# The query's low part on all 128 partitions: score products of two attentions in a two-layer trunk step

## The chip, the cores and the metric

The kernel runs on one core of a Trainium2 chip, as one launch. The metric is device time in microseconds (us), the median of three runs. Engines are named as the profile does: PE is TensorE's matrix products, PEld its loads of the stationary operand, DVE VectorE, ACT ScalarE, POOL GpSimd, SP the queue that issues the DMAs. L78 is line 78 of the kernel before.

## What is computed

One step through two layers of a diffusion backbone: 512 sample tokens and 128 prompt tokens, 1024 channels, float32. Each layer runs four token mixers side by side (a gated linear recurrence, grouped-query attention, neighbourhood attention, latent attention), merges them through gates, and ends in a feed-forward network. The change touches the scores of two of the mixers. Of the reference:

```python
# neighbourhood attention: 8 heads of 64, a window of the sample plus 256 cached keys
s_loc = jnp.einsum('brqhd,brjkhd->bhrqjk', qg, kg).astype(jnp.float32) * NA_SCALE
s_ctx = jnp.einsum('brqhd,bphd->bhrqp', qg, k_ctx).astype(jnp.float32) * NA_SCALE
...
# latent attention: 8 heads, 64 channels made from a latent and 32 rotary ones shared by the heads
k = jnp.concatenate([kv[..., :ML_NOPE],
                     jnp.broadcast_to(k_rope[:, :, None, :], (B, T, ML_HEADS, ML_ROPE))], axis=-1)
...
s = jnp.einsum('bqngd,bknd->bngqk', qblk, k).astype(jnp.float32) * scale
p = jax.nn.softmax(s, axis=-1).astype(v.dtype)
```

## The kernel before

**Two parts.** PE multiplies a rounded form of float32 (`F32R`), so every operand is kept as a high part (the rounded value) and a low part (what the rounding left). A projection is three products, `hi*hi`, `hi*lo` and `lo*hi`, summed in PSUM (`gemm`, and `part`, which gives it out in steps).

**Scores.** A head has 64 channels, half of the 128 partitions. `k_pair` (L480) keeps a head's keys as one tile `kp` (`nkp` in the neighbourhood attention, `mkp` in the latent one): high part on its own 64 partitions, low part on the other 64. `split_q` (L199) keeps the query's high part on both halves (`nqd`, `mqd`, one tile per head; the second half is a copy by DVE, L206), and the low parts of the two heads together in one tile (`nql`, `mqlo`): head A's on partitions 0 to 63, head B's on 64 to 127. `pair_scores` (L485) then makes two products per range of keys: the high part against both parts of the keys, a sum over 128 partitions, and the low part against the keys' high part, over 64. The latent attention adds a third, over 128 partitions, for the rotary channels (`kr`, `mqrr`). In grouped-query attention (`gkA`, `gq`) both products of a range of keys run over 128 partitions.

**An attention pair.** `attn_pair` (L243) works on two heads in nine units: the prompt of both heads, then per head four tiles of 128 queries. A unit's scores go to `pss`, the only buffer of its kind (two PSUM banks); DVE takes the maximum, ACT the exponential, DVE the division. Later steps transpose the probabilities on PE (`pst<-ident,P`), split them (`ph`, `pl`) and multiply by V. Neighbourhood units have 256 or 384 keys of the window and 256 cached ones, latent units 768 (512 and 256); the prompt unit has 128.

**Order.** A layer runs 16 such steps: four latent pairs, four recurrence heads, four neighbourhood pairs, four grouped-query pairs. `weave` (L1074) puts, between the steps of the pair under way, pieces of other work in proportion to given lengths: the preparation of the next pair (its projections and splits) and gates and merges (`psg` products). From what this program order says, the framework's scheduler makes the order of each engine, which holds at run time. `psg` has three buffers, `wraw` (weights as loaded) two.

**SBUF.** `Arena` hands out slots of two sizes, 38 of 640 columns and 19 of 896; of the free ones it takes the one that has been free longest, and a 640 tile takes a large slot when no small one is free. A tile in a reused slot waits for the last reader of the tile before it. No DMA is issued from POOL.

The lines that matter most:

```python
            self.split(q[a, cols], ql[a, cols], src[a], scale)          # split_q, per head
            self.nc.vector.tensor_copy(q[b, cols], self.r(q[a, cols]))
...
        self.mm(S[:, o : o + n], qd[half][:, qc], kp[half][:, k0 : k0 + n], True, False)
        self.mm(S[:, o : o + n], ql[a, qc], kp[half][a, k0 : k0 + n], False, last)
```

Of the kernel before, what the change touches and what calls it, by code (L numbers as in the profile page):

```python
# [8 lines left out]
F32R = mybir.dt.float32r  # L9
# [5 lines left out]
PSUM = bass.MemoryType.PSUM  # L15
# [5 lines left out]
GW = 64  # L21
# [13 lines left out]
class Arena:  # L35
    """Slots of SBUF handed out in program order, the longest free one first."""
# [28 lines left out]
class Trunk:  # L65
# [7 lines left out]
    # ---------------------------------------------------------------- basics  # L73
# [30 lines left out]
    def wload(self, src, a, b, joined=False, kept=None):  # L104
        """Both parts of a weight, each [128, a, b]; joined: side by side, [128, a, 2 b];
        kept: a list that gets the tiles, from the arena."""
# [20 lines left out]
    def gemm(self, w, xs, c0, c1, ms=slice(0, 128), k0=0):  # L127
        """PSUM [m, c1-c0] of one column range; xs = (hi, lo) tiles by k."""
        hi, lo = w
        m = ms.stop - ms.start  # L130
        ps = self.psg()
        o = ps[:m, 0 : c1 - c0]
        n = len(xs)
        for k in range(n):
            self.mm(o, hi[:, k0 + k, ms], xs[k][0][:, c0:c1], k == 0, False)
            self.mm(o, hi[:, k0 + k, ms], xs[k][1][:, c0:c1], False, False)
        for k in range(n):
            self.mm(o, lo[:, k0 + k, ms], xs[k][0][:, c0:c1], False, k == n - 1)
        return o

    def part(self, w, xs, c0, c1):
        """gemm, in steps of 8 products, negative: inside one product; the last step is the caller's."""
# [11 lines left out]
    def fm(self, src, name, scale=1.0):  # L154
        """Feature-major projection of one block of 128 columns, as float32."""
# [7 lines left out]
    def flip(self, t, c0, c1, rows=128):  # L163
        """Blocks of 128 columns c0..c1 of t transposed, side by side in PSUM."""
# [6 lines left out]
    # ------------------------------------------------------- splits into parts  # L171
    def split(self, hi, lo, src, scale=1.0):
        """hi = round(src*scale), lo = src*scale - hi."""
# [7 lines left out]
    def split_stack(self, dst, src, half, scale=1.0):  # L181
        """src rows of head `half` (64 partitions) -> dst stacked [hi;lo] or [lo;hi]."""
# [4 lines left out]
    def split_dup(self, dst, src, half, cols):  # L187
        """dst = (hi, lo), each on both halves of the partitions."""
# [10 lines left out]
    def split_q(self, qd, ql, src, cols, scale):  # L199
        """qd: per head, hi on both halves; ql: [lo A; lo B]."""  # L200
        for half in range(2):
            a = slice(64 * half, 64 * half + 64)
            b = slice(64 - 64 * half, 128 - 64 * half)
            q = qd[half]
            self.split(q[a, cols], ql[a, cols], src[a], scale)
            self.nc.vector.tensor_copy(q[b, cols], self.r(q[a, cols]))  # L206

    # ---------------------------------------------------------------- attention
    def softmax(self, S, P, p0, n1, n2, bias):
        """Probabilities of the scores S[:, 0:n1] (+ bias) and S[:, 512:512+n2] to P from  # L210
        column p0 on; the part that has a bias first when p0 says so."""
# [24 lines left out]
    def add_halves(self, dst, pv):  # L236
        """dst [64, n] = rows 0-63 of pv + rows 64-127."""
# [5 lines left out]
    def attn_pair(self, scores, plan, vst, frees):  # L243
        """Two heads, prompt and sample, in steps: the scores of one query tile, the transposes of
        the tile before, the products with V of the one before that; returns the output,
        feature-major. scores(S, half, t) writes the scores of query tile t; plan[g] = (V tiles by
        column of P, per query tile (first column, columns, ...)); frees[half] goes with the head."""
# [103 lines left out]
    def v_tile(self, vst, src, t0):  # L351
        """src [128 keys, n tiles x 2 heads x 64] -> V per head, [128 keys, tile, hi|lo]."""
# [6 lines left out]
    def v_split(self, vst, t, cache):  # L359
        """V of t, feature-major, and of the cache, token-major; tiles 0-3 sample, 4-5 cache, 6 prompt."""  # L360
# [17 lines left out]
    # ------------------------------------------------------------------- GQA  # L378
    def gqa_normed(self, l, blk, g, cost):
        """Block of two heads, token-major: normalised, gained, rotated (sample)."""  # L380
# [82 lines left out]
    def rope(self, out, x, nb, nf, cos, sin):  # L463
        """out, x [128, nb*2*nf], pairs interleaved; cos, sin [128, nb, nf]."""
# [14 lines left out]
    # ------------------------------------------------- neighbourhood attention  # L479
    def k_pair(self, kp, src, cols):  # L480
        """kp: head A [hi;lo], head B [lo;hi]."""
# [3 lines left out]
    def pair_scores(self, S, o, qd, ql, kp, half, qc, k0, n, last):  # L485
        a = slice(64 * half, 64 * half + 64)
        self.mm(S[:, o : o + n], qd[half][:, qc], kp[half][:, k0 : k0 + n], True, False)
        self.mm(S[:, o : o + n], ql[a, qc], kp[half][a, k0 : k0 + n], False, last)

    def na_pair(self, l, i, c):  # L490
# [21 lines left out]
        ql = self.u("nql", F32R)  # L512
# [23 lines left out]
        # P by columns: (cache, 0, 1, 2) and (1, 2, 3, cache)  # L536
        plan = (((4, 5, 0, 1, 2), ((0, 4, 256, 256, 256, 0), (0, 5, 384, 256, 256, 0))),
                ((1, 2, 3, 4, 5), ((0, 5, 384, 256, 0, 384), (1, 5, 256, 256, 128, 384))))
        frees = [[kp[0], vst[0], qd[0]], [kp[1], vst[1], qd[1], ql]]
        return lambda: self.attn_pair(scores, plan, vst, frees)  # L540

    # ------------------------------------------------------------------- MLA
    def mla_pre(self, l):
        """Compressed latents: normalised query latent, keys' latent, rotary parts."""
# [3 lines left out]
        # the projections, first columns of all first  # L548
        raw3 = [self.u("mfm") for _ in range(4)]
        for c0, c1 in HALVES:  # L550
# [4 lines left out]
            # both parts of the weights side by side  # L555
# [58 lines left out]
        # rotary key: rows [hi; hi; lo; lo]  # L614
# [27 lines left out]
        # rotary part of the queries, token-major  # L642
# [18 lines left out]
    def mla_pair(self, l, i, c):  # L661
# [5 lines left out]
        # rotary queries of the two heads, rows [hi; lo; hi; lo]  # L667
# [17 lines left out]
        ql = self.u("mqlo", F32R)  # L685
# [8 lines left out]
        if i % 2 == 0:  # L694
            # values of this pair and the next one
# [27 lines left out]
        frees = [[kp[0], vst[0], qd[0], qr[0]], [kp[1], vst[1], qd[1], qr[1], ql] + ([kr] if i == 3 else [])]  # L723
        return lambda: self.attn_pair(scores, FULL, vst, frees)

    # ------------------------------------------------------------------- HGRN
    def hgrn_head(self, l, h, c):
        nc, A = self.nc, self.A

        def evac(fn, dst, ps, c0, c1):  # L730
            """column order (col, row) of the sample -> row-major; prompt as it is."""
# [15 lines left out]
        # Blocks of w tokens, at first one. Per direction: T, the decay of each block; queries by the  # L747
        # decay since the block's edge; keys by that up to it. Kept by turns: of forward and backward
        # what the products of this level take, and the other one.
# [16 lines left out]
        # value, token-major in row order  # L766
# [6 lines left out]
        # output gate, feature-major in token order  # L773
# [12 lines left out]
    def hgrn_mix(self, l, h, Q, T, qs, ks, kk, v, sg):  # L786
        nc, A = self.nc, self.A
        blk = [slice(c * 128, (c + 1) * 128) for c in range(5)]
        # pair matrix At[s, t], level by level
# [10 lines left out]
        for lev in range(7):  # L800
# [7 lines left out]
            # of four blocks the outer ones keep their direction on the next level, the inner ones  # L808
            # change it; on the last level all blocks end up with one direction
# [24 lines left out]
        # T: [128, 5] decay of each chunk; states chunk by chunk  # L834
# [51 lines left out]
    # ------------------------------------------------------------------ merge  # L886
    def gate(self, l, n, d, gates, away=False):
        """tanh of half the gate, branch n, block d."""
# [29 lines left out]
    # ------------------------------------------------------------------ adaLN  # L918
    def silu(self, c):
        """silu of both conditions, kept as rows in DRAM."""  # L920
# [8 lines left out]
    def ada_first(self, c):  # L929
        """Blocks 0..15 of layer 0, weights moving; loads x and starts on the first columns' norm."""  # L930
# [15 lines left out]
    def ada_chunk(self, l, q, c):  # L946
        """Blocks 4q..4q+3 of layer l on TensorE, the weights moving."""
# [18 lines left out]
    def ada_tail(self, l, b0, b1, parts, depth, last=False):  # L966
        """Blocks b0..b1 of layer l, weights by channel, one part of the sum after the other:
        mod[l][:, b] = silu(cond) w + b."""
# [33 lines left out]
    # --------------------------------------------------------------- main norm  # L1002
    def rstd_rows(self, x, c0, c1):
        """x: 8 tiles; returns a tile [128, c1-c0], every row 1/rms of the tokens c0..c1."""
# [529 lines left out]
```

## Time and profile before

| | us |
|---|---|
| median of three runs (lowest, highest) | 3252.76 (3247.86, 3254.46) |
| the profiled execution, first to last instruction | 3253.3 |
| PE busy | 3155.2 (97%) |
| PEld busy | 2956.6 (91%) |
| DVE busy | 2179.9 (67%) |
| ACT busy | 1457.7 (45%) |
| POOL busy | 290.5 (9%) |

The profiled execution has no other time than its span; it lies 0.5 us above the median. Busy time is the union of an engine's instructions. Products on PE overlap, since one starts while the one before it drains, so what a product costs in a row of products is read from start to start, not from its duration. The span divides into stages, by the first and last score products: latent attention 128 to 360 us, recurrence to 634, neighbourhood attention to 865, grouped-query attention to 1080, then merge, output projection and feed-forward network; the second layer's four mixers stand at 1740, 1972, 2212 and 2443.

### The profile page before, as it was taken

The numbers are of one execution on the slowest core, as the hardware profiler recorded it, in microseconds if no ns is written. First come the engines' busy times: TensorE is split into PE (matmuls) and PEld (weight loads), VectorE is DVE, ScalarE is ACT, GpSimd is POOL, SyncE is SP. The second block draws the span as 40 slices with busy tenths as digits, with TensorE's granted clock in tenths as the row PEclk, the third lists the DMA queues.
The fourth block names the chain that finished last, engine by engine and source line by source line (L and its number), as shares of the span: only waits on it lengthen the run. The fifth ranks groups of instructions, "written<-read, shape, count | busy, mean of one in ns | idle before, by whom it ended". The sixth has DMA issues, their size and how long they took to land.

```text
span 3253.3 us, 54150 instructions
## 1 busy us (share of the span) xinstructions
PE 3155.2 (97%) x20898; PEld 2956.6 (91%) x20898; DVE 2179.9 (67%) x4830; ACT 1457.7 (45%) x3086; POOL 290.5 (9%) x301
## 2 busy tenths in 40 slices
PE   8999998999999999999999999999999999999998
PEld 4888988888889999999997889998888999999998
DVE  5675888877777577777867666677677766533334
ACT  4554433455666352121355544445566644422222
POOL 1100222110111010000001002231001100000000
PEclk9999999999999999999999999999999999999999
DMA  6111243232111345444521112213221124322222
GB/s 211 63 54 57 86 129 113 88 95 87 49 40 58 107 139 173 149 153 150 158 99 58 48 58 78 71 53 98 86 71 43 39 62 148 106 82 74 79 72 72
DMA packets 135121, 297.16 MB, mean 91 GB/s; under 512 B 15888, under 2 KB 53584, under 8 KB 134864
## 3 DMA queue, kind: packets, MB, share of 16 engines
q1 hardware_dynamic: 134864, 293.71, 28.6%
q8 instruction: 165, 2.70, 0.3%
q14 instruction: 92, 0.75, 0.1%
HBM read 276.70 MB, written 16.95 MB: 90 GB/s over the span
## 4 chain that ended last, share of the span: by engine, by line
PE 74%; DVE 10%; issue 10%; ACT 3%; DMA 2%; POOL 1%; DVEq 0%; POOLq 0%; SPq 0%; ACTq 0%
PE psg L78 57%; PE pss L78 10%; PE pst L78 3%; PE pst L81 3%; DVE trash L984 2%; DVE wlo L123 1%; PE pst L167 1%; DMA ada<-in_w_ada 1%; ACT P L234 1%; DVE hA L804 1%; DVE hq L819 0%; DVE pl L176 0%; DVE sm L217 0%; ACT ph L84 0%; DVE P L231 0%
## 5 line engine op out<-in xcount | busy, mean ns | idle before, releaser
L78 PE MATMUL psg<-hh,whi 128*128 128x384 f32 (+1 forms) x3776 | 1128.4, 317 | 5.9 <-ACT whi L84 2.8
L78 PE MATMUL psg<-hl,whi 128*128 128x384 f32 (+1 forms) x3776 | 1112.9, 312 | 4.4 <-DVE hl L1061 2.9
L78 PEld LDWEIGHTS psg<-hh,whi 128*128 128x128 f32 x3776 | 717.6, 190 | 13.5 <-ACT whi L84 3.2
L78 PEld LDWEIGHTS psg<-hl,whi 128*128 128x128 f32 x3776 | 717.8, 190 | 9.6 <-DVE hl L1061 5.0
L78 PE MATMUL psg<-hh,wlo 128*128 128x384 f32 (+1 forms) x3744 | 653.1, 314 | 0.0
L84 ACT ACTIVATE whi<-wraw 128x1024 fp32r<-128x1024 f32 (+3 forms) x402 | 380.0, 947 | 470.2 <-PE psg L78 387.3
L78 PEld LDWEIGHTS psg<-hh,wlo 128*128 128x128 f32 x3744 | 572.4, 191 | 2.2
L123 DVE TENSOR_TENSOR wlo<-wraw,whi 128x1024 fp32r<-128x1024 f32 (+3 forms) x398 | 452.6, 1138 | 125.7 <-ACT whi L84 113.0
L234 ACT ACTIVATE P<-pss,sm 128x768 f32<-128x768 f32 (+2 forms) x240 | 162.6, 679 | 226.2 <-DVE sm L217 130.4
L176 DVE TENSOR_TENSOR pl<-pst,ph 128x384 fp32r<-128x384 f32 (+2 forms) x408 | 196.1, 510 | 30.0 <-ACT ph L84 26.0
L84 ACT ACTIVATE ph<-pst 128x384 fp32r<-128x384 f32 (+2 forms) x408 | 169.8, 456 | 54.1 <-PE pst L81 50.9
L217 DVE TENSOR_REDUCE sm<-pss 128x1 f32<-128x768 f32 x128 | 122.1, 954 | 102.3 <-PE pss L78 101.7
L81 PE MATMUL pst<-ident,P 128*128 128x128 f32 x1104 | 167.3, 275 | 13.9 <-DVE of L241 11.1
L1070 DVE SCALAR_TENSOR_TENSOR xr<-psg,mod,xr 128x128 f32<-128x128 f32 (+1 forms) x192 | 78.5, 435 | 148.4 <-PE psg L78 148.4
L984 DVE CUSTOM_DVE_ANT_0 yada<-ada 128x512 f32<-128x512 f32 x224 | 154.3, 689 | 5.2
L78 PE MATMUL psg<-oTl,whi 128*128 128x384 f32 (+1 forms) x512 | 153.4, 315 | 0.3 <-DVE oTl L176 0.3
L78 PE MATMUL psg<-oTh,whi 128*128 128x384 f32 (+1 forms) x512 | 153.6, 318 | 0.0
L81 PEld LDWEIGHTS pst<-ident,P 128*128 128x128 f32 x1104 | 125.8, 140 | 28.1 <-DVE of L241 16.5
L78 PE MATMUL psg<-fh,whi 128*128 128x256 f32 (+1 forms) x512 | 148.3, 309 | 0.0
L78 PE MATMUL psg<-fl,whi 128*128 128x256 f32 (+1 forms) x512 | 148.2, 308 | 0.0
L84 ACT ACTIVATE fh<-fy 128x384 fp32r<-128x384 f32 (+1 forms) x88 | 41.5, 472 | 184.3 <-DVE fy L1211 184.3
L1211 DVE SCALAR_TENSOR_TENSOR fy<-ft,psg 128x384 f32<-128x384 f32 (+1 forms) x88 | 42.9, 487 | 120.5 <-PE psg L78 120.1
(322 smaller groups left out, 5219.9 us busy)
## 6 DMA issues: line engine op xcount, KB each, us to landing
wraw<-in_w_f SPq DMA_DIRECT2D x128, 512.0 KB, 3.4
wraw<-in_w_in SPq DMA_DIRECT2D x88, 512.0 KB, 3.4
wraw<-in_w_gate SPq DMA_DIRECT2D x64, 512.0 KB, 3.3
ada<-in_w_ada SPq DMA_DIRECT2D x112, 256.0 KB, 3.0
wraw<-in_w_br SPq DMA_DIRECT2D x64, 256.0 KB, 2.7
wraw<-in_w_out SPq DMA_DIRECT2D x32, 512.0 KB, 3.3
ada<-in_w_ada SPq DMA_DIRECT2D x96, 128.0 KB, 2.3
gd<-gt SPq DMA_DIRECT2D x28, 320.0 KB, 2.3
```

Source lines behind the costliest of these rows:

```text
L78: self.nc.tensor.matmul(out, lhsT, rhs, start=start, stop=stop)
L81: self.nc.tensor.transpose(out, in_, self.ident)
L84: self.nc.scalar.activation(out, in_, AF.Copy, scale=scale)
L123: nc.vector.tensor_sub(lo[:, :n], raw[:, :n], self.r(hi[:, :n]))
L167: self.nc.tensor.transpose(ps[:, i * rows : (i + 1) * rows], t[:rows, c0 + i * 128 : c0 + (i + 1) * 128], self.ident[:rows, :rows])
L176: self.nc.vector.tensor_sub(lo, src, self.r(hi))
L217: nc.vector.tensor_reduce(nm, S[:, 0:n], axis=AX.X, op=ALU.max, negate=True)
L234: self.nc.scalar.activation(P, S, AF.Exp, bias=nm, accum_out=l)
L804: nc.vector.copy_predicated(Am.rearrange("p (c t) -> p c t", c=5), self.hmask[:, lev].unsqueeze(1).broadcast_to([128, 5, 128]), S[:, 0:NT] ...
L984: nc.vector.tensor_tensor_reduce(out=y, in0=w, in1=c, scale=1.0, scalar=0.0, op0=ALU.mult, op1=ALU.add, accum_out=acc[:, b, k, j : j + 1])
L1070: self.nc.vector.scalar_tensor_tensor(x[:, a:b], ps[:, a - c0 : b - c0], mod[:, b_g + m, j : j + 1], x[:, a:b], op0=ALU.mult, op1=ALU.add)
L1211: nc.vector.scalar_tensor_tensor(y[:, 0:n], tg[:, 0:n], 0.5, pa, op0=ALU.mult, op1=ALU.mult)
```

## The change

The low part of the query gets a tile per head, with the same values on both halves of the partitions; DVE makes the second half by a copy, as it does for the high part. The second score product then runs over 128 partitions: low part of the query against high and low part of the keys (the sum gains the product of the two low parts, left out before). Each pair in preparation holds one more slot of 640 columns. The arena gets 44 small slots in place of 38, and the SBUF for them comes from scratch for POOL's DMAs, set to 1024 bytes. The rest of the diff takes out comments.

```diff
     def split_q(self, qd, ql, src, cols, scale):
-        """qd: per head, hi on both halves; ql: [lo A; lo B]."""
         for half in range(2):
             a = slice(64 * half, 64 * half + 64)
             b = slice(64 - 64 * half, 128 - 64 * half)
-            q = qd[half]
-            self.split(q[a, cols], ql[a, cols], src[a], scale)
+            q, z = qd[half], ql[half]
+            self.split(q[a, cols], z[a, cols], src[a], scale)
             self.nc.vector.tensor_copy(q[b, cols], self.r(q[a, cols]))
+            self.nc.vector.tensor_copy(z[b, cols], self.r(z[a, cols]))
...
     def pair_scores(self, S, o, qd, ql, kp, half, qc, k0, n, last):
-        a = slice(64 * half, 64 * half + 64)
         self.mm(S[:, o : o + n], qd[half][:, qc], kp[half][:, k0 : k0 + n], True, False)
-        self.mm(S[:, o : o + n], ql[a, qc], kp[half][a, k0 : k0 + n], False, last)
+        self.mm(S[:, o : o + n], ql[half][:, qc], kp[half][:, k0 : k0 + n], False, last)
...
-        ql = self.u("nql", F32R)
+        ql = [self.u("nql", F32R) for _ in range(2)]
...
-        frees = [[kp[0], vst[0], qd[0]], [kp[1], vst[1], qd[1], ql]]
+        frees = [[kp[0], vst[0], qd[0], ql[0]], [kp[1], vst[1], qd[1], ql[1]]]
...
-        ql = self.u("mqlo", F32R)
+        ql = [self.u("mqlo", F32R) for _ in range(2)]
...
-        frees = [[kp[0], vst[0], qd[0], qr[0]], [kp[1], vst[1], qd[1], qr[1], ql] + ([kr] if i == 3 else [])]
+        frees = [[kp[0], vst[0], qd[0], ql[0], qr[0]], [kp[1], vst[1], qd[1], ql[1], qr[1]] + ([kr] if i == 3 else [])]
...
-SLOTS = ((640, 38), (896, 19))
+SLOTS = ((640, 44), (896, 19))
...
-    nc = bacc.Bacc("TRN2", target_bir_lowering=False, num_devices=1)
+    nc = bacc.Bacc("TRN2", target_bir_lowering=False, num_devices=1, dynamic_dma_scratch_size=1024)
```

The order of instructions names results (128 queries by so many keys), not the partitions that a product sums over, so the widened products read as before in it. On DVE, at the query splits of the first latent pair of layer 0, stood before:

```order
L178 SCALAR_TENSOR_TENSOR mqlo<-psg,mqd 64x384
L206 CAST mqd<-mqd 64x384
L178 SCALAR_TENSOR_TENSOR mqlo<-psg,mqd 64x384
L206 CAST mqd<-mqd 64x384
L123 TENSOR_TENSOR wlo<-wraw,whi 128x256
L178 SCALAR_TENSOR_TENSOR mqlo<-psg,mqd 64x256
L206 CAST mqd<-mqd 64x256
L178 SCALAR_TENSOR_TENSOR mqlo<-psg,mqd 64x256
L206 CAST mqd<-mqd 64x256
```

and stands now:

```order
L178 SCALAR_TENSOR_TENSOR mqlo<-psg,mqd 64x384
L206 CAST mqd<-mqd 64x384
L207 CAST mqlo<-mqlo 64x384
L178 SCALAR_TENSOR_TENSOR mqlo<-psg,mqd 64x384
L206 CAST mqd<-mqd 64x384
L207 CAST mqlo<-mqlo 64x384
L178 SCALAR_TENSOR_TENSOR mqlo<-psg,mqd 64x256
L206 CAST mqd<-mqd 64x256
L207 CAST mqlo<-mqlo 64x256
L123 TENSOR_TENSOR wlo<-wraw,whi 128x256
```

One copy (L207) has come in behind each of the four splits, 64 copies in the program, and the low part of a weight (`wlo`, the latent pairs' value weights) has moved behind the third.

On PE, in the second latent pair of layer 0, at the scores of one query tile (`hh` and `hl` are the two parts of the layer's input, `whi` a weight):

```order
 L78 MATMUL psg<-hh,whi 128x256
 L78 MATMUL psg<-hl,whi 128x256
+L78 MATMUL psg<-hh,whi 128x256
+L78 MATMUL psg<-hl,whi 128x256
+L78 MATMUL pss<-mkp,mqd 128x512
 L81 MATMUL pst<-ident,P 128x128 x3
-L78 MATMUL psg<-hh,whi 128x256
-L78 MATMUL psg<-hl,whi 128x256
-L78 MATMUL pss<-mkp,mqd 128x512
 L78 MATMUL pss<-mkp,mqlo 128x512
 L78 MATMUL pss<-kr,mqrr 128x512
```

Three transposes of the tile before have moved behind the first score product; the score products themselves stand in the same order, and around most units of this stage nothing has moved.

On DVE at the start of the program, between the norm of the first 384 columns and that of the other 256 (`nacc`, sums of squares):

```order
 L961 SCALAR_TENSOR_TENSOR mod_123<-psg,bada 128x8
 L1013 TENSOR_TENSOR nacc<-nacc,nsq 128x384 x3
+L1013 TENSOR_TENSOR nacc<-nacc,nsq 128x256
 L961 SCALAR_TENSOR_TENSOR mod_123<-psg,bada 128x8
 L1022 RECIPROCAL rs<-rs 128x3
-L1027 TENSOR_SCALAR dg<-ident,rs 128x128 x3
+L1027 TENSOR_SCALAR dg<-ident,rs 128x128 x2
+L1013 TENSOR_TENSOR nacc<-nacc,nsq 128x256 x2
+L1027 TENSOR_SCALAR dg<-ident,rs 128x128
+L1013 TENSOR_TENSOR nacc<-nacc,nsq 128x256 x2
 L1054 SCALAR_TENSOR_TENSOR nx<-x_162,mod_123,nacc 128x384
 L1054 SCALAR_TENSOR_TENSOR nx<-x_164,mod_123,nacc 128x384
```

The sums of the second columns have come forward into the norm of the first. Such moves, by a few places, stand in many parts of the program.

## Rows read from the trace of the kernel before

**Rows 1.** The page: busy time, share of the span and instructions of the engines.

```profile
PE 3155.2 (97%) x20898; PEld 2956.6 (91%) x20898; DVE 2179.9 (67%) x4830; ACT 1457.7 (45%) x3086; POOL 290.5 (9%) x301
```

**Rows 2.** Stages: length; busy us (instructions) of PE, PEld, DVE, ACT, POOL; clock, DMA.

```profile
128.00:360.00 232.00, 228.53 (x1402) 195.18 (x1401) 154.15 (x327) 122.81 (x295) 4.69 (x3) 0.99 0.19 61
634.00:865.00 231.00, 228.06 (x1433) 203.14 (x1432) 168.25 (x478) 129.84 (x370) 18.83 (x17) 1.00 0.28 86
865.00:1080.00 215.00, 207.28 (x1449) 196.47 (x1448) 162.59 (x314) 132.05 (x273) 28.18 (x35) 1.00 0.15 47
360.00:634.00 274.00, 246.89 (x1717) 236.24 (x1717) 238.73 (x674) 107.13 (x207) 63.87 (x65) 0.97 0.34 104
```

**Rows 3.** Timeline of PE, scores of one latent query tile: start, duration, instruction.

```profile
139.50 0.40 PE L78 MATMUL pss<-mkp,mqd 128*128 128x512 f32 x1
139.82 0.50 PE L78 MATMUL pss<-mkp,mqlo 64*128 64x512 f32 x1
140.25 0.50 PE L78 MATMUL pss<-kr,mqrr 128*128 128x512 f32 x1
140.59 0.28 PE L78 MATMUL pss<-mkp,mqd 128*128 128x256 f32 x1
140.80 0.38 PE L78 MATMUL pss<-mkp,mqlo 64*128 64x256 f32 x1
141.11 0.39 PE L78 MATMUL pss<-kr,mqrr 128*128 128x256 f32 x1
141.33 0.71 PE L167 MATMUL pst<-ident,mst 128*128 128x128 f32 x5
```

**Rows 4.** Timeline of the weight loads beside them, with idle time before.

```profile
139.82 0.18 PEld L78 LDWEIGHTS pss<-mkp,mqlo 64*128 64x128 f32 x1 [0.31 <-issue]
140.25 0.19 PEld L78 LDWEIGHTS pss<-kr,mqrr 128*128 128x128 f32 x1 [0.25 <-issue]
```

**Rows 5.** Timeline of PE, scores of one grouped-query tile (512, 512, 256, 256).

```profile
935.70 0.87 PE L78 MATMUL pss<-gkA,gq 128*128 128x512 f32 x4
936.41 0.38 PE L167 MATMUL pst<-ident,gfm 128*128 128x128 f32 x2
```

**Rows 6.** Timeline of PE, scores of one neighbourhood query tile.

```profile
638.98 0.28 PE L78 MATMUL pss<-nkp,nqd 128*128 128x256 f32 x1
639.19 0.38 PE L78 MATMUL pss<-nkp,nql 64*128 64x256 f32 x1
639.50 0.38 PE L78 MATMUL pss<-nkp,nqd 128*128 128x256 f32 x1
...
640.12 0.38 PE L78 MATMUL psg<-hh,wlo 128*128 128x256 f32 x1
640.37 0.44 PE L81 MATMUL pst<-ident,P 128*128 128x128 f32 x2
```

**Rows 7.** Timeline of PE: projections of 256 columns, and into 64 output rows.

```profile
127.44 0.28 PE L78 MATMUL psg<-whi,ckvl 128*128 128x256 f32 x1
127.56 0.28 PE L78 MATMUL psg<-whi,ckvh 128*128 128x256 f32 x1
...
62.11 0.33 PE L78 MATMUL psg<-hh,whi 128*64 128x384 f32 x1
62.28 0.34 PE L78 MATMUL psg<-hl,whi 128*64 128x384 f32 x1
```

**Rows 8.** Instructions by tile, the 64-partition products: count, min/median/max ns, forms.

```profile
L78 PE MATMUL pss<-mkp,mqlo x144: 323/382/503, 128.1 to 1967.8; 64*128 64x512 f32 x64, 64*128 64x256 f32 x64, 64*128 64x128 f32 x16
...
L78 PE MATMUL pss<-nkp,nql x144: 322/381/443, 634.8 to 2437.9; 64*128 64x256 f32 x96, 64*128 64x384 f32 x32, 64*128 64x128 f32 x16
```

**Rows 9.** Timeline of PE, scores of a neighbourhood prompt unit.

```profile
634.79 0.32 PE L78 MATMUL pss<-nkp,nql 64*128 64x128 f32 x1
...
635.55 0.44 PE L78 MATMUL psg<-oTh,whi 128*128 128x384 f32 x1
```

**Rows 10.** Instructions of line 206, the copies of the high part.

```profile
L206 DVE CAST mqd<-mqd x32: 287/322/357, 119.8 to 1885.9; 64x384 fp32r<-64x384 f32 x16, 64x256 fp32r<-64x256 f32 x16
```

## The prediction

> **What bounds the kernel now.** I read the page first. PE is busy 97% of the span, no other engine over 67%, PEld apart, which feeds it [rows 1]. A share over two layers hides where the change acts, so I cut the span into its stages. In the latent attention of layer 0 PE is busy 228.53 of 232 us, in the neighbourhood attention 228.06 of 231, with DVE at 154.15 and 168.25; the granted clock is 0.99 and 1.00 of 2.4 GHz [rows 2]. So in the two stages that are touched PE has 3.5 and 2.9 us of idle time, and what shortens its work shortens the stage, as long as DVE (66 and 73%) can follow. The second layer's two stages have the same lengths.
>
> Busy time on PE is not work, though: a product's duration holds its drain. So I went to the timeline and read from start to start. Products of 256 columns follow each other at 0.12 us, those of 384 at 0.17 [rows 7]. A latent score block is different: the 64-partition product starts 0.32 after the 512-column product ahead of it, the next one 0.43 later, the one after that 0.34; at 256 columns the steps are 0.21, 0.31 and 0.22 [rows 3]. Six products take 1.83 us (139.50 to 141.33). The twin without a 64-partition product is the grouped-query block, 512, 512, 256, 256: 935.70 to 936.41, 0.71 us [rows 5], so 0.355 for a 512 and a 256 together.
>
> The weight loads say why. The load for the 64-partition product, and the load for the 128-partition one behind it, start with their own product's start (139.82, 140.25), after 0.31 and 0.25 us in which PEld waited for nothing that the trace shows [rows 4]. Elsewhere each product has its load too (1402 and 1401 in the first of [rows 2]), and at a pitch of 0.12 it isn't seen [rows 7]. I read it so: going from 128 partitions to 64, and back, PE takes up neither the next weights nor the next product until what runs is through. It is the number of partitions summed over, not of output rows: projections into 64 rows (128\*64) keep the pitch of 0.17 at 384 columns [rows 7].
>
> **The change, term by term.**
>
> *Latent score blocks.* There are 64 with 512 and 256 columns [rows 8]. At the grouped-query pitch six products take 3 × 0.355 = 1.06 us; 1.83 − 1.06 = 0.77 saved, × 64 = 49 us.
>
> *Neighbourhood score blocks.* Also 64: 96 products of 256 columns and 32 of 384, two to a block [rows 8]. From the first product of a block to the second instruction behind it 638.98 to 640.37 = 1.39 us go by for five products of 256 columns, since the product behind the block still pays for the way back (640.12 to 640.37, 0.25) [rows 6]. At 0.12 they take 0.60; 0.79 × 64 = 51 us. For the blocks with a 384 product I take the same, since the loss is per change of height.
>
> *Prompt units.* 32 products of 128 columns [rows 8]. Two low-part products and the high-part one between them, 634.79 to 635.55, take 0.76 for three [rows 9]; at no more than 0.12 each that is 0.40 saved for two, and I take 0.2 to 0.27 each, 8 us.
>
> The sum is 49 + 51 + 8 = 108 us, or 0.37 for each of the 288 products. The widened product itself costs nothing more: the same columns stream, and the high-part product of the same block is just as high.
>
> *The copies.* 64 more copies on DVE, two per head and pair: the kind is there already, at a median of 0.322 us [rows 10], so 20.6 us of DVE, about 5 per stage. They belong to the preparation of the next pair, which runs beside the present pair's units; what hides them is DVE's idle time, 78 us in a latent and 63 in a neighbourhood stage [rows 2]. Queued behind each copy are the next head's split and softmax work of the present unit, delayed by a third of a microsecond. I put them at 0 on the path; without that cover they cost 20.6.
>
> *What comes back.* With the stall gone the stages have less spare time per unit. `pss` is single, so PE can't write the next scores before ACT has read these, and the fill between two units is now all that covers this round. The grouped-query stage is the measure: the same softmax, DVE at 76%, and PE idle for 7.7 of 215 us, 3.6% [rows 2]. A latent stage would go to about 205 us with DVE at (154 + 5) / 205 = 78%; 3.6% of 205 is 7.4, against 3.2 now on average. I take that for all four stages: 4 × 4.2 = 17 us given back. The bounds are 0 (the spare time stays as it is) and, if a neighbourhood stage is held by DVE (below), some 20 more.
>
> *Slots and order.* Six more slots of 640 columns mean later reuse and fewer waits for old readers, everywhere; and the scheduler's order moves by a few places in many parts, as at the start, where 6 sums of squares come in front of the first normalised tiles on DVE, and in the second latent pair, where three transposes moved behind a score product. The trace of before can't price a slot that it doesn't have. The nearest row is the recurrence stage of layer 0, in which PE idles 27 of 274 us beside a DVE busy for 239 [rows 2]: a tenth of the program's 98 us of PE idle time (3253.3 less 3155.2 [rows 1]), won or lost, is 10 us. I take 0 and keep ±10. No DMA is issued from POOL, so the smaller scratch costs nothing.
>
> Together: 3253.3 − 108 + 17 = 3162 us for the profiled execution; it lies 0.5 above the median, so 3161.5 for the median, 2.8% less.
>
> **The rivals.**
>
> *DVE takes over.* In the neighbourhood stage DVE would have 168 + 5 = 173 us of work in some 207 us, 84%. At 87%, in layer 0's recurrence stage, PE idles for a tenth [rows 2]. If the softmax chains can't be packed over 80% the stage stays at 217, ten more than the sum has it, and a latent stage, at 159 / 0.80 = 199, is still free: 20 us less gain, and with the copies a few more, about 3185. For it: 84% would be the highest share of DVE in an attention stage. Against: the grouped-query stage keeps PE at 96% beside a DVE at 76%, and layer 0's recurrence still keeps it at 90% beside one at 87%.
>
> *All of it passes.* Spare time stays as it is and the slots give something: 3253 − 108 − 10 = 3135.
>
> *The load stays in the open.* The stall could be that of any score product whose weights are new against a new buffer, so that at 128 partitions too the load is paid, 0.31 per 256 columns as now; then nothing is saved and the time stays at 3253. Against it stand the grouped-query block, with a load for each product, and the high-part products 0.12 behind a projection [rows 5, 7]. The Trainium skill has a rule that would bring this about ("TensorE: Matmul & The Clock Gate", Part 3, "The mechanism"): a weight load overlaps a running product only when the two are in different row groups. By that rule products over all 128 partitions could never hide a load, and the change would even take away the case in which one can. The trace disagrees where it counts: at one and the same set of 128 partitions the pitch is 0.12 with a load before every product, and it is the change of partitions that shows the load.
>
> *Slower.* The copy for head A stands on DVE between the two heads' splits, and both read one projection in `psg`, of which there are three buffers; each of the 32 column ranges holds its buffer for two copies, 0.64 us, longer. If PE waited for all of that, it is 20.6 us, 3274. It decides only if the change of height costs PE less than 20.6 / 288 = 0.07 us per low-part product; rows 3 and 6 show five times as much, so it needs the rival before it as well.
>
> **How the numbers follow.** The forecast, a saving of 108 with about 17 given back, has 0.77; DVE taking over 0.12; all of it 0.06; the load in the open 0.03; slower 0.02. The likeliest gives 3161. Its own bounds are 3135 (nothing given back, 10 from the slots) and 3253 − 108 + 17 + 20.6 + 10 = 3193 (copies in full on the path, the order 10 worse), which cover the second and third case too; both ends need everything to fall one way, so I give 3137 to 3190. A measurement of this kernel tells some 0.2%, 6.5 us, from no change. Faster by more: 0.77 + 0.12 + 0.06 = 0.95; within: 0.03; slower: 0.02.
>
> **What would show it.** Right: low-part products at 128\*128, score blocks of about 1.06 us (latent) and of 0.48 to 0.58 plus a plain product behind (neighbourhood); weight loads of these blocks no longer starting with their product; latent and neighbourhood stages of some 204 to 212 us; all other stages within a few us; 64 copies at line 207 of about 0.32 us. Wrong: a pitch that stays at 0.31 for 256 columns; or a right pitch with PE idle for over 15 us in a stage, waiting for `pss` readers or DVE; or a recurrence or feed-forward stage that moves by more than 10 us, which would be the slots and the order.

## The result and the profile after

The changed kernel takes 3160.56 us (median of four, 3157.4 to 3162.43) against 3252.14 for the kernel before: a ratio of 0.972, 95% interval 0.971 to 0.973. The profiled execution spans 3158.8 us.

The page of the changed kernel, first line of its busy times, answers to [rows 1]:

```profile
PE 3042.6 (96%) x20898; PEld 2934.2 (93%) x20898; DVE 2183.3 (69%) x4894; ACT 1467.5 (46%) x3090; POOL 286.0 (9%) x301
```

PE does the same 20898 products and is busy 112.6 us less (3155.2 − 3042.6), while the span fell by 94.5. The difference is idle time: 3158.8 − 3042.6 = 116.2 us now, 98.1 before, 18.1 more. Not all of the 112.6 is the products' own: the mean granted clock of PE was 0.994 in this execution and 0.991 in the one before, and 3253.3 × 0.009 less 3158.8 × 0.006 is an estimated 10 us, give or take 3, since the clock is given to three digits. DVE has 64 instructions more and is busy 3.4 us longer.

Timeline of PE, scores of a latent query tile, the changed kernel (compare [rows 3]):

```profile
138.84 0.39 PE L78 MATMUL pss<-mkp,mqd 128*128 128x512 f32 x1
139.07 0.40 PE L78 MATMUL pss<-mkp,mqlo 128*128 128x512 f32 x1
139.31 0.40 PE L78 MATMUL pss<-kr,mqrr 128*128 128x512 f32 x1
139.54 0.27 PE L78 MATMUL pss<-mkp,mqd 128*128 128x256 f32 x1
139.65 0.28 PE L78 MATMUL pss<-mkp,mqlo 128*128 128x256 f32 x1
139.77 0.28 PE L78 MATMUL pss<-kr,mqrr 128*128 128x256 f32 x1
139.89 0.71 PE L167 MATMUL pst<-ident,mst 128*128 128x128 f32 x5
```

The reader is to look at the starts: 0.23 or 0.24 apart at 512 columns, 0.11 or 0.12 at 256, and 1.05 us from the first product to what follows, where it was 1.83.

Timeline of the weight loads there (compare [rows 4]):

```profile
138.67 0.19 PEld L78 LDWEIGHTS pss<-mkp,mqd 128*128 128x128 f32 x1
138.84 0.19 PEld L78 LDWEIGHTS pss<-mkp,mqlo 128*128 128x128 f32 x1
139.07 0.19 PEld L78 LDWEIGHTS pss<-kr,mqrr 128*128 128x128 f32 x1
```

The load for the low-part product starts at 138.84, with the product ahead of it and 0.23 us before its own; no idle time is listed with it any more.

Timeline of PE, scores of a neighbourhood tile with 256 and 256 keys (compare [rows 6]):

```profile
627.98 0.28 PE L78 MATMUL pss<-nkp,nqd 128*128 128x256 f32 x1
628.10 0.28 PE L78 MATMUL pss<-nkp,nql 128*128 128x256 f32 x1
628.22 0.28 PE L78 MATMUL pss<-nkp,nqd 128*128 128x256 f32 x1
628.34 0.28 PE L78 MATMUL pss<-nkp,nql 128*128 128x256 f32 x1
628.46 0.52 PE L78 MATMUL psg<-oTh,wlo 128*128 128x256 f32 x3
```

Four products in 0.48 us, the pitch of any projection. The block before took 1.14 to the next product and 1.39 with that.

Stages of layer 0, each from the first product of its mixer into `pss` to the first of the next, the grouped-query stage to the first product of the output projection (latent, neighbourhood, grouped-query, then recurrence). The kernel before:

```profile
127.90:367.20 239.30, 235.83 (x1461) 202.47 (x1459) 161.13 (x349) 126.87 (x303) 4.69 (x3) 0.99 0.20 63
634.60:870.00 235.40, 230.83 (x1449) 205.34 (x1448) 172.63 (x487) 131.97 (x375) 21.75 (x22) 1.00 0.27 84
870.00:1127.10 257.10, 251.00 (x1754) 240.57 (x1754) 183.88 (x343) 146.11 (x293) 25.25 (x29) 1.00 0.19 59
367.20:634.60 267.40, 240.29 (x1665) 229.55 (x1663) 232.42 (x655) 103.27 (x200) 63.87 (x65) 0.97 0.34 104
```

and the changed one:

```profile
127.90:344.70 216.80, 209.54 (x1460) 200.63 (x1459) 164.13 (x359) 128.79 (x304) 6.89 (x5) 0.99 0.21 70
607.40:828.10 220.70, 210.39 (x1487) 203.58 (x1487) 174.23 (x501) 137.61 (x381) 21.64 (x22) 1.00 0.28 87
828.10:1081.80 253.70, 248.70 (x1726) 237.22 (x1725) 183.72 (x343) 144.64 (x291) 24.81 (x29) 1.00 0.18 56
344.70:607.40 262.70, 237.31 (x1655) 227.33 (x1653) 230.97 (x662) 101.89 (x198) 61.62 (x63) 0.97 0.35 108
```

The latent stage lost 22.5 us. The neighbourhood stage lost only 14.7, but it holds 38 products more (1487 for 1449), taken over from its neighbours (1726 for 1754, 1655 for 1665), which became 3.4 and 4.7 shorter. PE's idle time grew from 3.5 to 7.3 and from 4.6 to 10.3 us in the two touched stages.

### The profile page after: what moved, and what is told of

It reads as the page before. It is cut to its first block, busy times and chain, and to the rows that moved or that the text cites. A ratio compares the mean times of both kernels' runs of the same rounds, so it can differ in the third digit from the quotient of the medians.

```text
span 3158.8 us, 54167 instructions
## 1 busy us (share of the span) xinstructions
PE 3042.6 (96%) x20898; PEld 2934.2 (93%) x20898; DVE 2183.3 (69%) x4894; ACT 1467.5 (46%) x3090; POOL 286.0 (9%) x301
## 4 chain that ended last, share of the span: by engine, by line
PE 71%; DVE 15%; ACT 5%; issue 4%; DMA 4%; POOL 1%; SPq 0%; DVEq 0%; ACTq 0%; POOLq 0%
PE psg L78 58%; PE pss L78 7%; PE pst L81 3%; PE pst L78 3%; DVE wlo L123 2%; DVE trash L984 2%; ACT P L235 1%; DVE pl L176 1%; DMA ada<-in_w_ada 1%; ACT whi L84 1%; DVE nx L1054 1%; DMA wada<-in_w_adak 1%; PE pst L167 1%; DVE sm L218 1%; DVE P L232 1%
## 5 line engine op out<-in xcount | busy, mean ns | idle before, releaser
L81 PEld LDWEIGHTS pst<-ident,P 128*128 128x128 f32 x1104 | 125.6, 140 | 31.2 <-DVE of L242 17.6
```

The lines of the kernel that those rows point to most:

```text
L81: self.nc.tensor.transpose(out, in_, self.ident)
```

## The experiments

Times are medians; ratios are to the kernel before on the same chip, whose median was 3251 to 3254, with their 95% intervals.

**Slots alone.** On the kernel before:

```diff
-SLOTS = ((640, 38), (896, 19))
+SLOTS = ((640, 44), (896, 19))
...
-    nc = bacc.Bacc("TRN2", target_bir_lowering=False, num_devices=1)
+    nc = bacc.Bacc("TRN2", target_bir_lowering=False, num_devices=1, dynamic_dma_scratch_size=1024)
```

> The kernel before with 44 small slots and the small scratch, nothing else. Theory: in the changed kernel the stages that the score products don't touch came out about 10 us shorter in sum, and that is the work of the slots (later reuse, fewer waits, another order), so this kernel takes 3242 us, give or take 4. Rival: the shorter stages came from the order that the whole change happened to give; then this kernel lies within 4 us of 3252.

3243.74 us, ratio 0.9968 (0.9956 to 0.9981): 10.4 us, as the theory had it in size. Its page:

```profile
PE 3145.2 (97%) x20898; PEld 2950.1 (91%) x20898; DVE 2172.4 (67%) x4830; ACT 1465.0 (45%) x3090; POOL 288.2 (9%) x301
```

At a span of 3242.2 PE idles for 97.0 us, 1.1 less than before, and is busy 10.0 us less with the same products. So these are not the fewer waits that the theory names. What differs is the granted clock: 0.994 to 0.995 in these five runs, 0.991 to 0.993 in the fifteen of the kernel before beside them; 3253.3 × 0.009 less 3242.2 × 0.006 is 10 us, give or take 3. What PE does at the lower of the clock's two levels (1.2 and 2.4 GHz) stands in the timeline of the kernel before, in its feed-forward network, after a row of short waits:

```profile
1209.49 0.46 PE L78 MATMUL psg<-hl,whi 128*128 128x256 f32 x1 [0.68 <-DVE hl L1061]
...
1210.81 1.91 PE L78 MATMUL psg<-hh,wlo 128*128 128x256 f32 x8
1212.52 0.41 PE L78 MATMUL psg<-hh,whi 128*128 128x256 f32 x1
...
1214.67 1.11 PE L78 MATMUL psg<-hh,wlo 128*128 128x256 f32 x8
1215.62 0.28 PE L78 MATMUL psg<-hh,whi 128*128 128x256 f32 x1
```

Eight products of 256 columns take 1.71 us at a granted clock of 0.50 and 0.95 at 1.00. The kernel before shows the same between its own runs: on one chip (the last three experiments) 3252.9 to 3254.4 us at a mean clock of 0.991 and 3247.53 at 0.994. Why the clock was higher with 44 slots is not shown. Its stages, recurrence, neighbourhood and grouped-query of layer 0:

```profile
366.80:628.70 261.90, 238.20 (x1654) 229.14 (x1653) 227.47 (x654) 101.93 (x198) 62.60 (x63) 0.97 0.35 107
628.70:868.80 240.10, 235.51 (x1486) 210.44 (x1486) 173.95 (x491) 137.65 (x381) 22.17 (x22) 1.00 0.26 81
868.80:1122.60 253.80, 248.76 (x1726) 237.23 (x1725) 183.72 (x343) 144.55 (x291) 24.85 (x29) 1.00 0.18 56
```

These are the changed kernel's product counts, to within one. So the fill that the neighbourhood stage took over comes from the slots, not from the wider products, and it lengthens that stage by 4.7 us while the two beside it shorten by 5.5 and 3.3.

**Rows alone.** On the kernel before, with its 38 slots, one shared tile for the low parts and no copy. The sum is changed: the half of the partitions that belongs to the other head brings that head's low part against this head's low keys.

```diff
-        self.mm(S[:, o : o + n], ql[a, qc], kp[half][a, k0 : k0 + n], False, last)
+        self.mm(S[:, o : o + n], ql[:, qc], kp[half][:, k0 : k0 + n], False, last)
```

> The kernel before with 38 slots, no copies and one tile for the low parts of both heads; only the second score product runs over all 128 partitions (so it adds, in place of the own head's low part times the keys' low part, the other head's low part times this head's low keys; that part of the sum is changed). Theory: change of height costs PE some 110 us, of which about 28 come back as idle time in the four stages because the fill is all that covers the softmax round; without the copies and the slots that gives 3252 - 112 + 28 = 3168. Rival: what came back in the neighbourhood stages was DVE's load from the copies; then some 10 to 15 less comes back here, 3155. Third: the widening isn't what saves; then 3252.

3157.6 us, ratio 0.9708 (0.9695 to 0.9722): 95 us by the ratio, and as fast as the changed kernel. It lies between the theory (3168) and its rival (3155), nearer to the rival. The page:

```profile
PE 3047.2 (97%) x20898; PEld 2937.3 (93%) x20898; DVE 2174.8 (69%) x4830; ACT 1457.3 (46%) x3086; POOL 290.5 (9%) x301
```

At a span of 3154.7, PE is busy 108.0 us less than before and idle for 107.5, 9.4 more. The clock was 0.992, by which an estimated 4 of the 108.0 us are the clock's (3253.3 × 0.009 less 3154.7 × 0.008). The latent and neighbourhood stages of layer 0:

```profile
127.30:340.50 213.20, 207.59 (x1460) 199.60 (x1459) 159.28 (x349) 127.13 (x303) 4.71 (x3) 1.00 0.22 70
606.40:820.40 214.00, 205.37 (x1449) 198.21 (x1449) 171.42 (x488) 131.77 (x375) 21.77 (x22) 1.00 0.29 92
```

With the same 1449 products as before the neighbourhood stage is down by 21.4 us, the latent one by 26.1.

**Copies alone.** The changed kernel, its second product again over 64 partitions:

```diff
-        self.mm(S[:, o : o + n], ql[half][:, qc], kp[half][:, k0 : k0 + n], False, last)
+        a = slice(64 * half, 64 * half + 64)
+        self.mm(S[:, o : o + n], ql[half][a, qc], kp[half][a, k0 : k0 + n], False, last)
```

> The changed kernel with its two tiles, its copies and its 44 slots, but the second score product again over 64 partitions. Theory: the copies hide behind PE, so this takes what the slots alone take, within 4 us. Rival: the copies are on the path, then 10 to 20 us more than the slots alone, 3252 to 3262.

3250.88 us, ratio 0.9992 (0.9983 to 1.0001), against 0.9968 for the slots alone: 0.0024 × 3252 = 7.8 us more with the copies, although PE was still stalling. By the time the theory that they hide fell, and the rival, 10 to 20, had it too high. The page:

```profile
PE 3152.8 (97%) x20898; PEld 2956.4 (91%) x20898; DVE 2188.6 (67%) x4894; ACT 1467.1 (45%) x3090; POOL 286.4 (9%) x301
```

At a span of 3249.5 PE idles for 96.7 us, slots alone for 97.0: it does not wait for the copies. It is busy 7.6 us longer with the same products, at a clock of 0.992 for 0.994, which makes some 6 of it. So a cost of the copies' own is not shown here; it shows where PE no longer stalls (below).

**Grouped.** On the kernel before, 64-partition products kept, but each unit's low-part products side by side at its end:

```diff
-        self.mm(S[:, o : o + n], qd[half][:, qc], kp[half][:, k0 : k0 + n], True, False)
-        self.mm(S[:, o : o + n], ql[a, qc], kp[half][a, k0 : k0 + n], False, last)
...
+        for o, n, k0 in ranges:
+            self.mm(S[:, o : o + n], qd[half][:, qc], kp[half][:, k0 : k0 + n], True, False)
+            if rot:
+                self.mm(S[:, o : o + n], rot[0][half][:, qc], rot[1][:, k0 : k0 + n], False, False)
+        for o, n, k0 in ranges:
+            self.mm(S[:, o : o + n], ql[a, qc], kp[half][a, k0 : k0 + n], False, True)
...
```

> The kernel before with 64-partition products, but the low-part products of a unit side by side at its end (high and rotary products of both key ranges first): two changes of height per unit in place of four. Theory (loss per change of height, about 0.2 us each way): the 256 wide products lose half, about 50 us less, 3200 to 3205 if little comes back. Rival (loss per low-part product, whatever stands beside it, as a load that stays in the open would have it): within 8 us of 3252.

3203.39 us, ratio 0.9842 (0.9826 to 0.9857): 51 us less, half of what the rows alone give, as the theory had it. The timeline of one latent block:

```profile
140.07 0.39 PE L78 MATMUL pss<-mkp,mqd 128*128 128x512 f32 x1
140.30 0.40 PE L78 MATMUL pss<-kr,mqrr 128*128 128x512 f32 x1
140.53 0.28 PE L78 MATMUL pss<-mkp,mqd 128*128 128x256 f32 x1
140.65 0.28 PE L78 MATMUL pss<-kr,mqrr 128*128 128x256 f32 x1
140.86 0.61 PE L78 MATMUL pss<-mkp,mqlo 64*128 64x512 f32 x2
141.40 0.77 PE L167 MATMUL pst<-ident,mst 128*128 128x128 f32 x5
```

Two low-part products in a row take 0.54 us with the way back, 0.19 more than a 512 and a 256 at plain pitch (0.35), and the way in shows as 0.21 for the 256-column product ahead of them (140.65 to 140.86). Their loads:

```profile
140.86 0.29 PEld L78 LDWEIGHTS pss<-mkp,mqlo 64*128 64x128 f32 x2
```

One such load takes 0.18 [rows 4], both together 0.29, so the second starts while the first product runs. The second pays nothing that shows: the loss belongs to the change of height, not to the product of 64 partitions.

**One mixer.** The changed kernel with the latent attention's low-part product at 64 partitions:

```diff
-        self.mm(S[:, o : o + n], ql[half][:, qc], kp[half][:, k0 : k0 + n], False, last)
+        a = slice(0, 128) if last else slice(64 * half, 64 * half + 64)
+        self.mm(S[:, o : o + n], ql[half][a, qc], kp[half][a, k0 : k0 + n], False, last)
```

> The changed kernel, widened in the neighbourhood attention only; the latent attention's low-part product runs over 64 partitions again (copies and slots stay). Theory: the slots are worth 10, the copies cost some 7, and of the 57 us that the neighbourhood stages lose at changes of height about 42 stay gained: 3251 less 42, 3209, so that the latent half of the change is worth about 47. Rival: idle time passes from one stage to another and the two halves don't add; then this lies over 6 us off 3209.

3207.62 us, ratio 0.9858 (0.9844 to 0.9871). By the ratios, widening the neighbourhood attention is worth (0.9992 − 0.9858) × 3252 = 44 us, and the latent one on top (0.9858 − 0.9719) × 3252 = 45. These two sum to the whole by the way they are taken; that the halves do add is seen in the stages. Layer 0's neighbourhood stage takes 221.8 us here (627.3 to 849.1), 220.7 in the changed kernel and 243.5 in copies alone (627.5 to 871.0); its latent stage takes 238.4 (126.1 to 364.5), as in copies alone (125.6 to 364.0), and 216.8 in the changed kernel.

**Copies on POOL.** The changed kernel with

```diff
-            self.nc.vector.tensor_copy(z[b, cols], self.r(z[a, cols]))
+            self.nc.gpsimd.tensor_copy(z[b, cols], self.r(z[a, cols]))
```

> The changed kernel with the 64 copies of the low part on POOL in place of DVE. Theory (the copies cost by standing in DVE's queue among the softmax work): 7 to 15 us less than the changed kernel, 3146 to 3155. Rival (what came back in the neighbourhood stages is the short fill around the single score buffer, not DVE): within 4 us of 3161.

3158.59 us, ratio 0.9706 (0.9693 to 0.9719), 4 us by the ratios under the changed kernel with overlapping intervals: less than the theory's 7 to 15, and where the rival had it. Its page:

```profile
PE 3043.5 (96%) x20898; PEld 2937.0 (93%) x20898; DVE 2169.9 (69%) x4830; ACT 1466.9 (46%) x3090; POOL 325.8 (10%) x365
```

At a span of 3154.8 PE idles for 111.3 us, 4.9 less than in the changed kernel, though the copies themselves take longer on POOL, 632 and 520 ns at the median against 316 on DVE (the profile's spans on POOL are rough). Its clock was 0.991 to 0.992 and the changed kernel's 0.993 to 0.994, an estimated 3 to 9 us to this run's disadvantage, so the ratio alone doesn't settle what the move is worth.

**Zero half.** The changed kernel without copies; four fixed tiles whose other half is zero, and 40 small slots, since the fixed tiles take the room of four:

```diff
-            self.nc.vector.tensor_copy(z[b, cols], self.r(z[a, cols]))
...
-        ql = [self.u("nql", F32R) for _ in range(2)]
+        ql = self.low()
...
-SLOTS = ((640, 44), (896, 19))
+SLOTS = ((640, 40), (896, 19))
```

> The changed kernel without copies: four fixed tiles (two per head, by turns) hold the low part on the head's own half, and the other half is set to zero once at the start; 40 small slots beside them. The sum is then the one of the kernel before. Theory: rows alone gave 3158 and the slots 10, so with copies gone 3147 to 3151. Rival: the fixed tiles wait for the pair before the last and cost what the copies did; then 3158 or more.

3168.2 us, ratio 0.9741 (0.9727 to 0.9756): a miss, 8 us slower than the changed kernel. Its five runs had a clock of 0.989 (3176.44 us) to 0.993 (3163.49), the changed kernel's 0.993 to 0.994, so much of the 8 us can be the clock. Its latent and recurrence stages of layer 0:

```profile
127.30:339.70 212.40, 207.34 (x1460) 199.44 (x1460) 155.00 (x314) 126.90 (x301) 4.67 (x3) 1.00 0.20 66
339.70:616.50 276.80, 244.56 (x1684) 232.68 (x1683) 239.14 (x696) 105.57 (x207) 64.22 (x65) 0.98 0.36 108
```

The latent stage is the shortest of all these runs, so no pair is seen to wait there for the fixed tiles, which was the rival's reason, though the time is one that it allowed (3158 or more). The recurrence stage is long, 276.8 us where 38 slots gave 267.4 and 44 gave 261.9 to 262.7. In part that is work moved into it, 1684 products for 1665 and 1655; but PE also idles longer there, 32.2 us for 27.1 before and 25.4 in the changed kernel. That 40 slots should be worse than both has no cause that I could show; it stays open.

**Rows and slots.** Rows alone with 44 slots and the small scratch, so the changed kernel less its copies and second tile (the sum changed as in rows alone).

> The kernel with one shared tile for the low parts and the product over all 128 partitions (rows alone: that part of the sum is changed as there), and 44 slots besides; it differs from the changed kernel by the copies and the second tile alone. Theory: rows (96) and slots (10) add, 3147, so that the copies cost the changed kernel some 14 us. Rival: with PE's stall gone the slots have nothing left to give; then 3157, and the copies cost 4.

3153.54 us, ratio 0.9694 (0.9681 to 0.9707), between the two expectations: the slots add 0.0014 × 3252 = 5 us to the rows, not 10, and the copies cost (0.9719 − 0.9694) × 3252 = 8. The page:

```profile
PE 3041.2 (96%) x20898; PEld 2934.2 (93%) x20898; DVE 2169.3 (69%) x4830; ACT 1464.5 (46%) x3090; POOL 288.0 (9%) x301
```

At a span of 3151.6 PE idles for 110.4 us: 2.9 more than in rows alone, so the slots took no wait away here either (the clock was 0.994 for 0.992), and 5.8 less than in the changed kernel, which is what the copies cost in idle time.

**The changed kernel again, and copies made twice.** On one chip:

```diff
             self.nc.vector.tensor_copy(z[b, cols], self.r(z[a, cols]))
+            self.nc.vector.tensor_copy(z[b, cols], self.r(z[a, cols]))
```

> The changed kernel once more, so that the two beside it stand against it on the same chip: a ratio of 0.972 to before, 3160 to 3163.

> The changed kernel with each of the 64 new copies made twice (128 copies, 20 us more of DVE). Theory: leaving the copies out gave 7 to 9 us (rows and slots against the changed kernel), so each set costs that: 3168 to 3172. Rival: those 9 us were another order and not the copies' time; then within 4 us of the changed kernel.

3160.03 us (ratio 0.972, 0.9706 to 0.9733) and 3173.43 (0.9763, 0.975 to 0.9777). The second set costs 13.4 us of the 64 × 0.316 = 20 that it is busy, a little over the theory's 3168 to 3172; the rival falls. The two pages:

```profile
PE 3043.8 (96%) x20898; PEld 2933.3 (93%) x20898; DVE 2182.0 (69%) x4894; ACT 1467.7 (46%) x3090; POOL 286.8 (9%) x301
PE 3049.6 (96%) x20898; PEld 2934.6 (93%) x20898; DVE 2206.2 (70%) x4958; ACT 1466.5 (46%) x3090; POOL 285.4 (9%) x301
```

At spans of 3158.6 and 3170.3 PE idles for 114.8 and 120.7 us, 5.9 more with the second set. The other 5.8 of the 11.7 us between the spans are PE busy time, with no product more. The clock, 0.993 for 0.994, can be some 3 of it; a drain that counts as busy where nothing follows at once can be another part, which no run separates.

**All copies on POOL.** Rows and slots, with the kernel's older copies of the high part moved as well:

```diff
-            self.nc.vector.tensor_copy(q[b, cols], self.r(q[a, cols]))
+            self.nc.gpsimd.tensor_copy(q[b, cols], self.r(q[a, cols]))
```

> Rows and slots without the new copies (one shared tile for the low parts, 44 slots, the low keys meeting the other head's low part) and the 64 copies of the high part, which the kernel before has already, on POOL in place of DVE. Theory: a set of copies on DVE costs 4 to 9 us, so this is 4 to 9 less than rows and slots, 3145 to 3150, and the fastest so far. Rival: with the low copies gone DVE has enough spare time; then 3152 to 3156.

3148.04 us, ratio 0.9687 (0.9673 to 0.97), against 3160.03 for the changed kernel on the same chip: the fastest version here, 12 us under the changed kernel. Its scores hold the foreign low-part term of rows alone. Its time lies in the theory's 3145 to 3150; but against rows and slots, run on another chip, it gained 0.0007 × 3252 = 2 us by the ratios, under the theory's 4 to 9, and the intervals overlap. The page:

```profile
PE 3039.4 (97%) x20898; PEld 2936.3 (93%) x20898; DVE 2146.2 (68%) x4766; ACT 1465.8 (47%) x3090; POOL 325.1 (10%) x365
```

At a span of 3145.5 PE idles for 106.1 us, 4.3 less than in rows and slots. So the older copies cost PE some 4 us of idle time; what they cost in time is not settled.

## Why the prediction was right

The forecast was 3161 and the median is 3160.56. The mechanism held; that it came within 1 us is luck. The widening gave some 104 us for 108, a higher clock gave an estimated 10 that no term had, and PE's idle time rose by 18.1 us for the 17 given back, but of these 9.4 came with the rows, 2.9 with the slots and 5.8 with the copies, which had been put at 0.

*The stall at a change of height.* Shown. Blocks fell to 1.05 and 0.48 us, the loads run ahead again, and with half the changes of height half the gain came (grouped), which a cost per 64-partition product can't do. The sum had 108 us; the rows alone took 108.0 off PE's busy time, and less the clock's share of about 4 that is 104, or 0.36 us for each of the 288 products.

*The load in the open.* Fallen. The rule of the Trainium skill ("TensorE: Matmul & The Clock Gate", Part 3, "The mechanism") that a load passes a running product only in another row group is, taken by itself, not what this chip did: the low part's load at 138.84 runs beside a product on the same 128 partitions. The same section also lets a load go ahead into the background weight buffer, which leaves room for that.

*What comes back.* 17 was forecast, for the fill and the single score buffer. Rows alone gave back only 9.4. For the cause that the prediction named, 17 was about double. The reading "as idle as the grouped-query stage" put 4.2 on every stage; with rows alone the latent stage has 2.1 more idle time (5.6 for 3.5) and the neighbourhood stage 4.1 (8.6 for 4.6). How much of that is the single buffer was not tried with a second one.

*The copies, put at 0.* The step that failed: "what hides them is DVE's idle time". In time the first set cost 8 us beside the widening (rows and slots against the changed kernel) and a second set 13, between the bounds of 0 and 20.6. What they do is clearest in PE's idle time, with wide products and 44 slots, by the number of sets of 64 copies on DVE (the set of the high part counts as one):

| kernel | sets on DVE | PE idle, us |
|---|---|---|
| all copies on POOL | 0 | 106.1 |
| rows and slots | 1 | 110.4 |
| copies on POOL | 1 | 111.3 |
| the changed kernel, profiled twice | 2 | 116.2, 114.8 |
| copies made twice | 3 | 120.7 |

Each set on DVE costs PE 4 to 6 us of idle time, and a set moved to POOL, where a copy takes longer, doesn't. Two profiles of one kernel differ by 1.4 here, so the steps are clear of that. So it is the time in DVE's queue that costs, and not that a copy is made; that it is the softmax steps of the present unit that wait behind it was not separated from DVE's other work. With PE still stalling the copies added no idle time (96.7 for 97.0 us).

*Slots and order, put at 0 within 10.* They gave 10 alone and 5 beside the rows, inside the bounds, but not by the reason given, "later reuse and fewer waits": PE's idle time went from 98.1 to 97.0 alone and from 107.5 to 110.4 beside the rows, and the gain went with a clock of 0.994 for 0.991 and 0.992. The slots also moved 38 products into the neighbourhood stage, which is why that stage gained least: 14.7 off the prediction's 231 us is 216, over its 204 to 212.

*DVE taking over.* The changed neighbourhood stage has DVE at 79% (174.23 of 220.70), near the 80% that this rival named; with the product count of before (rows alone) it is 214.0 us at 80%. No neighbourhood stage shown here has DVE at more, so whether 80% is a ceiling stays open. But PE is busy for 205.37 of those 214.00 us, so DVE held the stage by 8.6 us at most.

## What to carry to other kernels

A product over fewer partitions than its neighbours cost PE the overlap on both sides here, 0.36 us for each; widen it if the operand can be had for less, or else put such products side by side. Read the pitch from start to start and look where the weight load starts: a load that starts with its own product is the sign. And price a short copy on a busy in-order engine by what waits behind it, not by that engine's idle share. Where two kernels differ by a few microseconds, compare PE's busy time, its idle time and the granted clock before calling the difference a wait.

## What the chip showed that I had not expected

Each set of 64 copies on DVE, busy 68 to 70% of the span, added 4 to 6 us of idle time on PE, which was busy for 96%, and the same copies on POOL did not, although one takes 520 to 632 ns at the median there and 316 on DVE. And six more slots made the kernel 10 us faster with PE's idle time as it was: the same 20898 products took 10.0 us less, at a mean granted clock of 0.994 for 0.991.
